# The low-half matmul of logits and index scores on 128 rows of the partitions

## The chip, the cores and the metric

The kernel runs on one core of one Trainium2 chip. The metric is the device time of one execution in microseconds (us); lower is better. The engines are called as in the profile: PE is the matmul engine (TensorE) and PEld its weight loads, DVE is VectorE, ACT is ScalarE, POOL is GpSimd, SP is the engine that issues most DMAs.

## The reference, cut to what matters

One decoder layer over x of 512 tokens by 2048. One input projection feeds three mixers and their gates; then an output projection, a LayerNorm, a gated convolution MLP and a second LayerNorm. All of it is float32.

- DSA: 8 heads of 64. An indexer with 16 heads of 64 scores every query against every earlier key: the sum over heads of weight x relu(query . key). The 128 greatest scores of a row select the keys that the softmax may use.
- S5: a diagonal state space scan over 32 groups, then a gated linear unit.
- MoBA: 8 heads of 64. At this length each query sees its own block of 256 and all past ones, so it is a causal softmax.
- Both softmaxes add a T5 relative bias, one row of a table for each head and distance.

```
rel    = relu(einsum('bqhd,bsd->bqhs', q_idx, k_idx))
score  = einsum('bqh,bqhs->bqs', w_idx, rel)
logits = einsum('bqhd,bshd->bhqs', q, k) * scale + bias
```

## The kernel before

Every matrix product runs in float32r with operands split in two: v = h + l, where h is v rounded to float32r (written by ScalarE) and l = v - h (written by VectorE). A full product is three matmuls, h.h + h.l + l.h (`mm3`, L91 to L93).

Heads of 64 leave half of the 128 partitions free, and the kernel uses them for a shorter form. `q_stacks` makes for a pair of heads the tiles sa and sb: in one half of the partitions the high half of a query, in the other its low half. `k_stacks` makes ka and kb, in which the high half of a key stands on both halves of the partitions, so that one matmul over 128 rows gives h.h + l.h. The remaining h.l is a second matmul over 64 rows into the same bank: only the half of the stack that holds the high half of the query, against the low half of the key in the tile kl. kl holds the low half of head A on partitions 0 to 63 and that of head B on 64 to 127.

`logits` does this for one head and four query tiles of 128 tokens, which see 128, 256, 384 and 512 keys (L438, L440). In DSA a third matmul adds the mask of the selected keys in bf16 (L442), except for the first tile. Each result lies in a bank of the ring "at" (3 banks), is reduced with the bias strip by VectorE (L444) and exponentiated by ScalarE (L446). The strips come by a DMA from a table in DRAM, fdr, that `t5_rows` writes once, when the S5 stage has given its memory free.

`dsa_index` does the same for 16 index heads and three query tiles (L641, L642). All of them share one key, which stands in kia (high half, on both halves of the partitions) and kil (low half, on both halves as well).

The tiles of `q_stacks` and `k_stacks`, and the inputs of S5, share a ring, qp, of six tiles [128, 512]. A pair of softmax heads takes five of them: sa, sb, ka, kb, kl.

The stages follow each other: input transposes, the projections of DSA and S5, index scores, selection of keys (`dsa_topk`, on VectorE), S5, MoBA, DSA, branch products and gates, output projection, MLP. Gate products are put between the parts of the mixers (`gates_ahead`), so that PE has work while the other engines have the mixers'. A planner orders each engine's instructions ahead of the run, from estimated durations and priorities; at run time each engine takes its own in that order. Weights stream on SP's queue; their splits have raised priority.

Of the kernel before, what the change touches and what calls it, by code (L numbers as in the profile page):

```python
# [9 lines left out]
F32 = mybir.dt.float32  # L10
F32R = mybir.dt.float32r
# [5 lines left out]
DRAM = bass.MemoryType.DRAM  # L17
RIGHT = "right"

P = 128  # L20
T = 512
# [7 lines left out]
BIG = 1e30  # L29
HP = 2000  # L30
WK = 11
# gates computed ahead after each part of the mixers
# [7 lines left out]
def tile_trunk(ctx: ExitStack, tc: tile.TileContext, x, rel_bias, w_in, cq_gain, ckv_gain,  # L40
# [3 lines left out]
    nc = tc.nc  # L44
# [50 lines left out]
    # W as the stationary operand: out[col tile] = W[:, cols]^T @ X^T, 512 tokens wide  # L95
# [16 lines left out]
    # 128 columns at the same place of both halves of a matrix's columns  # L112
# [37 lines left out]
    def s5_pow_e(pool, y, name):  # L150
        # e^y to the last bit or so: y = k ln2 + r, a polynomial in r, 2^k from the exponent bits
        sh = list(y.shape)
        n_ = [0]

        def tl(dt=F32):
            n_[0] += 1
            return pool.tile(sh, dt, tag=f"pe{n_[0]}", name=f"pe{n_[0]}")
        v = nc.vector
        yc, k, r, p, e = tl(), tl(), tl(), tl(), tl()
        ki = tl(mybir.dt.int32)  # L160
        v.tensor_scalar(yc, y, -87.0, 88.0, op0=ALU.max, op1=ALU.min)
        v.tensor_scalar(k, yc, 1.4426950408889634, 12582912.0, op0=ALU.mult, op1=ALU.add)
        v.tensor_scalar(k, k, -12582912.0, None, op0=ALU.add)
        v.scalar_tensor_tensor(r, k, -0.693359375, yc, op0=ALU.mult, op1=ALU.add)
        v.scalar_tensor_tensor(r, k, 2.12194440054690583e-4, r, op0=ALU.mult, op1=ALU.add)
        v.tensor_scalar(p, r, 1.0 / 5040, None, op0=ALU.mult)
        for c in (1.0 / 720, 1.0 / 120, 1.0 / 24, 1.0 / 6, 0.5, 1.0):
            v.scalar_tensor_tensor(p, p, c, r, op0=ALU.add, op1=ALU.mult)
        v.tensor_scalar(k, k, 127.0, 8388608.0, op0=ALU.add, op1=ALU.mult)
        v.tensor_copy(ki, k)  # L170
        v.scalar_tensor_tensor(e, p, 1.0, ki.bitcast(F32), op0=ALU.add, op1=ALU.mult)
        return e

    s5 = mside.enter_context(ExitStack())
    sp = right(s5, "sp")
    lhsB = sp.tile([96, 4, 2, 4, P], F32R, name="lhsB")      # h, h, l; q, re/im, G, state
# [9 lines left out]
    def s5_params():  # L186
        v = nc.vector
# [26 lines left out]
        # sine and cosine by half angles after reduction to [-pi, pi]  # L214
# [28 lines left out]
        # (lam_bar - 1) / lam  # L243
# [22 lines left out]
        # input matrices, block-diagonal over the two groups of a pair, inputs on partitions  # L266
# [27 lines left out]
        # output matrices with the states on partitions  # L294
# [12 lines left out]
        # e^{i theta t}, t < 32  # L307
# [59 lines left out]
    fdr = dr.tile([16, 23, 640], F32, name="fdr")  # L367

    def t5_rows():
        with tc.using_default_side(RIGHT), tc.tile_pool(name="t5", bufs=1, reuse_waits="tile") as t5:  # L370
            oh = t5.tile([32, 640], F32, name="oh")
            nc.sync.dma_start(oh, onehot)
            rb = t5.tile([32, 16], F32, name="rb")
            nc.sync.dma_start(rb, rel_bias)
            fr = t5.tile([16, 640], F32, name="fr")
            tb = tp_bank()
            nc.tensor.matmul(tb[:16, :512], rb, oh[:, 0:512], start=True, stop=True)
            nc.vector.tensor_copy(fr[:, 0:512], tb[:16, :512])
            nc.vector.memset(fr[:, 512:640], BIG)
            # 23 copies of a row, so that steps of one row less 1 or 16 elements walk back in distance  # L380
            nc.sync.dma_start(fdr, fr[:, None, :].to_broadcast([16, 23, 640]))

# [17 lines left out]
    def k_stacks(bank):  # L400
        ka = qp.tile([P, T], F32R, tag="q", name="ka")
        kb = qp.tile([P, T], F32R, tag="q", name="kb")
        kl = qp.tile([P, T], F32R, tag="q", name="kl")
        nc.scalar.activation(ka[0:64], bank[0:64], AF.Copy)
        nc.scalar.activation(kb[64:128], bank[64:128], AF.Copy)
        nc.vector.tensor_sub(kl[0:64], bank[0:64], ka[0:64].bitcast(F32))
        nc.vector.tensor_sub(kl[64:128], bank[64:128], kb[64:128].bitcast(F32))
        nc.vector.tensor_copy(ka[64:128], ka[0:64].bitcast(F32))
        nc.vector.tensor_copy(kb[0:64], kb[64:128].bitcast(F32))
        return ka, kb, kl  # L410

    def v_store(bank, t):
        # bank [128 tok, 256 = (pair, A/B, 64)]
        src = bank.rearrange("p (a c d) -> p a c d", a=2, c=2)
        nc.scalar.activation(vh[:, t, :, 0::2, :], src, AF.Copy)
        nc.vector.tensor_sub(vl[:, t, :, 0::2, :], src, vh[:, t, :, 0::2, :].bitcast(F32))
# [3 lines left out]
    def logits(head, hd, qs, kst, mask):  # L420
        # normalised softmax rows of one head, the four query tiles side by side
        ka, kb, kl = kst
        s = qs[hd]
        kk = (ka, kb)[hd]
        half = slice(64 * hd, 64 * hd + 64)
# [8 lines left out]
        for i in range(NT):  # L434
            W = P * (i + 1)
            lb = at_bank()
            qi = slice(i * P, (i + 1) * P)
            nc.tensor.matmul(lb[:, :W], s[:, qi], kk[:, :W], start=True, stop=False)  # L438
            mk = mask is not None and i > 0
            nc.tensor.matmul(lb[:, :W], s[half, qi], kl[half, :W], start=False, stop=not mk)  # L440
            if mk:
                nc.tensor.matmul(lb[:, :W], identb, mask[i], start=False, stop=True)  # L442
            p_ = pt[:, POFF[i]:POFF[i] + W]
            nc.vector.tensor_tensor_reduce(p_, lb[:, :W], strip[:, 384 - i * P:384 - i * P + W],  # L444
                                           1.0, 3e38, ALU.add, ALU.min, mn[:, i:i + 1])
            nc.scalar.activation(p_, p_, AF.Exp, bias=mn[:, i:i + 1], scale=-1.0,  # L446
                                 accum_out=sm[:, i:i + 1])
# [36 lines left out]
    def u_split(G):  # L484
        # the stacked rows h, l, h of a pair of groups meet h, h, l of its matrices
        h, l = w2k("uh", dt=F32R), w2k("ul", dt=F32R)
        split(h, l, oT[1, G])
        us = [qp.tile([P, T], F32R, tag="q", name="us") for _ in range(4)]
        for q in range(4):
            for j, t_ in enumerate((h, l, h)):  # L490
                nc.sync.dma_start(us[q][32 * j:32 * j + 32].bitcast(F32), t_[32 * q:32 * q + 32].bitcast(F32))
        return us

    def s5_tile(G):
# [44 lines left out]
        # 2 gelu(y) in its tanh form  # L539
# [7 lines left out]
    def s5_glu():  # L547
        # 4 times the branch's output: (2 gelu) * (1 + tanh(z/2))
# [24 lines left out]
    def rms_apply(banks, gains, dst, width):  # L573
        # dst = c * gain * (mean(c^2) + eps)^-0.5; the mean token-major, then spread over the partitions
# [25 lines left out]
    def dsa_in():  # L600
# [6 lines left out]
        # index keys on both partition halves; index weights token-major  # L607
# [14 lines left out]
    # value at (p, m) stands for the distance p + 384 - m  # L622
# [5 lines left out]
    def dsa_index(gs):  # L628
        wq2 = w_qidx[0].rearrange("r h d -> r (h d)")
        for g in gs:  # L630
            banks = gemm_w(wq2, (256 * g, 256 * g + 256), cqT, kq=3)
            for pr in range(2):
                qs = q_stacks(banks[pr], 0.125)
                for hd in range(2):
                    h = 4 * g + 2 * pr + hd
                    half = slice(64 * hd, 64 * hd + 64)
                    for i in range(1, NT):
# [4 lines left out]
                        nc.tensor.matmul(lb[:, :W], qs[hd][half, qi], kil[half, :W], start=False, stop=True)  # L642
# [6 lines left out]
    def dsa_topk():  # L649
        # exactly the 128 greatest scores of a row, the lower index first among equals  # L650
# [48 lines left out]
    def moba_v(g):  # L699
        # two token tiles share a bank: its flags are cleared once, by the first of them  # L700
# [42 lines left out]
    qp = mx.enter_context(tc.tile_pool(name="qp", bufs=6, reuse_waits="tile"))  # L743
# [77 lines left out]
    # merged (gates carried twice the sigmoid)  # L821
# [47 lines left out]
    for c, (c0, n) in enumerate(CH):  # L869
# [14 lines left out]
        # the last columns token tile by token tile, so that LayerNorm follows behind  # L884
# [47 lines left out]
    # the accumulator of the down projection starts as alpha * x1  # L932
# [20 lines left out]
    def up_tile(j):  # L953
        if j == 0:
            # in token halves, the first ready before the second
# [37 lines left out]
    def down_last(grp, acts):  # L993
        # token tile by token tile, LayerNorm 2 behind each
# [59 lines left out]
def _bucket_onehot():  # L1054
    # -1 at the T5 bucket of the distance 511 - column (32 buckets, greatest distance 128)
# [32 lines left out]
```

## Time and profile before

| | |
|---|---|
| runs of the kernel before | 2831.72, 2834.8, 2835.8 us; median 2834.8 |
| profiled execution | span 2832.9 us from first to last instruction; no other time of its own is on record |
| mean granted clock of PE | 0.994 of full speed |
| PE busy | 2792.6 us, 99% |
| VectorE busy | 1449.3 us, 51% |
| ScalarE busy | 889.5 us, 31% |
| GpSimd busy | 224.5 us, 8% |

Matmuls overlap: a matmul's recorded duration reaches from its start to its modelled end, past the start of the next. What a stream of matmuls costs is therefore read from the distances between starts. The granted clock is a share of full speed; 0.5 is the lower of its two levels.

### The profile page before, as it was taken

What the parts mean: (1) busy time and instruction counts of PE and PEld (TensorE: products, weight loads), DVE (VectorE), ACT (ScalarE), POOL (GpSimd) and SP (SyncE); (2) the same over time, 40 slices, a digit from 0 to 9 for tenths busy, and PEclk for the clock granted to TensorE, in tenths of its full rate; (3) what the DMA queues carried; (4) which work ended last, traced back from release to release, by engine and by line L of the source; (5) the groups of instructions that cost most, each with busy time, mean ns of one, the idle gap of its engine ahead of it and who ended that gap; (6) DMA issues with size and microseconds to landing.
All of it is one profiled execution on the core that took longest, in us unless ns stands there. A gap on an engine that the chain in (4) does not pass through costs nothing.

```text
span 2832.9 us, 32264 instructions
## 1 busy us (share of the span) xinstructions
PE 2792.6 (99%) x12651; PEld 2255.8 (80%) x12655; DVE 1449.3 (51%) x2176; ACT 889.5 (31%) x1325; POOL 224.5 (8%) x163
## 2 busy tenths in 40 slices
PE   9999999999999999999899999999999999999998
PEld 7777877777887778889778888888888888888886
DVE  6357988885445446434553334333433333333448
ACT  3243333334344432212532232331322322322321
POOL 0000011110000003100420000000000000000002
PEclk9999999999999999999999999999999999999999
DMA  6223433334332335533433333333333333323333
GB/s 199 84 80 93 127 108 118 117 89 93 82 98 86 96 126 192 168 119 105 134 104 97 97 97 92 99 94 94 97 97 97 97 97 97 97 90 97 97 97 112
DMA packets 352824, 301.82 MB, mean 107 GB/s; under 512 B 20963, under 2 KB 307600, under 8 KB 352160
## 3 DMA queue, kind: packets, MB, share of 16 engines
q1 hardware_dynamic: 339536, 281.44, 33.2%
q10 hardware_dynamic: 10832, 14.12, 1.4%
q0 software_dynamic: 2304, 4.20, 0.6%
q8 instruction: 99, 1.62, 0.2%
q14 instruction: 53, 0.43, 0.0%
HBM read 278.31 MB, written 18.24 MB: 105 GB/s over the span
## 4 chain that ended last, share of the span: by engine, by line
PE 94%; DVE 3%; DMA 1%; issue 1%; POOL 1%; ACT 0%; DVEq 0%; SPq 0%; ACTq 0%; POOLq 0%
PE mmb L91 24%; PE mmb L93 23%; PE mmb L92 23%; PE atb L93 4%; PE atb L92 4%; PE atb L91 4%; PE avb L93 2%; PE avb L91 2%; PE avb L92 2%; PE atb L440 1%; PE atb L642 1%; PE atb L460 1%; PE mmb L711 1%; PE avb L536 1%; PE mmb L712 1%
## 5 line engine op out<-in xcount | busy, mean ns | idle before, releaser
L73 DVE TENSOR_TENSOR wl<-raw,wh 128x1024 fp32r<-128x1024 f32 (+1 forms) x468 | 601.1, 1285 | 946.6 <-ACT wh L72 930.2
L72 ACT ACTIVATE wh<-raw 128x1024 fp32r<-128x1024 f32 (+1 forms) x468 | 489.1, 1045 | 1364.1 <-PE mmb L92 905.0
L91 PE MATMUL mmb<-x1h,wh 128*128 128x512 f32 (+1 forms) x1440 | 552.7, 385 | 5.4 <-ACT wh L72 5.4
L92 PE MATMUL mmb<-x1l,wh 128*128 128x512 f32 (+1 forms) x1440 | 555.5, 386 | 1.6 <-DVE x1l L917 1.6
L93 PE MATMUL mmb<-x1h,wl 128*128 128x512 f32 (+1 forms) x1440 | 526.1, 385 | 6.8 <-DVE wl L73 6.8
L91 PE MATMUL mmb<-xh,wh 128*128 128x512 f32 (+1 forms) x1056 | 419.6, 398 | 1.2 <-ACT wh L72 1.2
L92 PE MATMUL mmb<-xl,wh 128*128 128x512 f32 (+1 forms) x1056 | 418.9, 397 | 0.0
L93 PE MATMUL mmb<-xh,wl 128*128 128x512 f32 (+1 forms) x1056 | 407.5, 397 | 0.6 <-DVE wl L73 0.6
L93 PEld LDWEIGHTS mmb<-x1h,wl 128*128 128x128 f32 x1440 | 270.9, 188 | 61.6 <-DVE wl L73 8.0
L91 PEld LDWEIGHTS mmb<-x1h,wh 128*128 128x128 f32 x1440 | 270.0, 188 | 60.0 <-ACT wh L72 6.3
L92 PEld LDWEIGHTS mmb<-x1l,wh 128*128 128x128 f32 x1440 | 271.3, 188 | 56.8 <-DVE x1l L917 2.6
L91 PEld LDWEIGHTS mmb<-xh,wh 128*128 128x128 f32 (+1 forms) x1056 | 199.3, 189 | 54.7 <-issue 9.0
L93 PEld LDWEIGHTS mmb<-xh,wl 128*128 128x128 f32 (+1 forms) x1056 | 198.7, 188 | 52.7 <-issue 9.4
L92 PEld LDWEIGHTS mmb<-xl,wh 128*128 128x128 f32 (+1 forms) x1056 | 199.1, 189 | 47.4 <-issue 6.9
L93 PE MATMUL atb<-wh,al 128*128 128x512 f32 x480 | 189.8, 395 | 0.0
L92 PE MATMUL atb<-wl,ah 128*128 128x512 f32 x480 | 189.5, 395 | 0.0
L949 DVE SCALAR_TENSOR_TENSOR cv<-mmb,cwc,cv 128x511 f32<-128x511 f32 (+1 forms) x176 | 131.6, 748 | 88.0 <-ACT cv L947 84.8
L91 PE MATMUL atb<-wh,ah 128*128 128x512 f32 x480 | 170.7, 395 | 0.0
L970 POOL TENSOR_TENSOR cv<-cv 128x512 f32<-128x512 f32 x44 | 57.7, 1311 | 1251.7 <-DVE cv L949 1251.7
L93 PEld LDWEIGHTS atb<-wh,al 128*128 128x128 f32 x480 | 89.9, 187 | 22.1
L91 PEld LDWEIGHTS atb<-wh,ah 128*128 128x128 f32 x480 | 90.0, 187 | 21.9
L92 PEld LDWEIGHTS atb<-wl,ah 128*128 128x128 f32 x480 | 90.0, 187 | 21.7
(369 smaller groups left out, 3342.6 us busy)
## 6 DMA issues: line engine op xcount, KB each, us to landing
raw<-in_w_up_dram SPq DMA_DIRECT2D x360, 256.0 KB, 3.4
raw<-in_w_in_dram SPq DMA_DIRECT2D x120, 512.0 KB, 3.7
raw<-in_w_down_dram SPq DMA_DIRECT2D x88, 512.0 KB, 3.6
raw<-in_w_out_dram SPq DMA_DIRECT2D x32, 512.0 KB, 3.7
raw<-in_w_branch_dram SPq DMA_DIRECT2D x24, 512.0 KB, 4.6
thd<-th ACTq DMA_DIRECT2D x22, 512.0 KB, 2.9
th<-thd SPq DMA_DIRECT2D x22, 512.0 KB
raw<-in_w_in_dram SPq DMA_DIRECT2D x32, 256.0 KB, 3.4
```

What stands on the lines that cost most here:

```text
L72: nc.scalar.activation(wh, raw, AF.Copy)
L73: nc.vector.tensor_sub(wl, raw, wh.bitcast(F32))
L91: nc.tensor.matmul(o, ah, bh, start=start, stop=False)
L92: nc.tensor.matmul(o, ah, bl, start=False, stop=False)
L93: nc.tensor.matmul(o, al, bh, start=False, stop=stop)
L440: nc.tensor.matmul(lb[:, :W], s[half, qi], kl[half, :W], start=False, stop=not mk)
L460: nc.tensor.transpose(tb[:, (i - j) * P:(i - j + 1) * P], pt[:, o:o + P], ident)
L536: nc.tensor.matmul(yb[rw], ctr[:, G, rw], t[0], start=True, stop=False, tile_position=(0, 32 * q))
L642: nc.tensor.matmul(lb[:, :W], qs[hd][half, qi], kil[half, :W], start=False, stop=True)
L711: nc.tensor.matmul(o, xh[:, ts_], wl[:, k], start=False, stop=False, skip_group_check=True)
L949: nc.vector.scalar_tensor_tensor(c_[:, s_:], bank[:, :T - s_], cwc[:, j * 88 + f:j * 88 + f + 1], c_[:, s_:], op0=ALU.mult, op1=ALU.add)
L970: nc.gpsimd.tensor_mul(ca, ca, cv)
```

## The change

The low half of the key is put on both halves of the partitions too. In `k_stacks`, kl becomes two tiles, la and lb, each filled on its second half by one more copy on VectorE. The second matmul of each logit then takes the whole stack of the query, over 128 rows, against la or lb. The second matmul of each index score takes the whole stack against kil, which already stands on both halves. So l.l is added to each product as well. The ring qp gets a seventh tile. The remaining lines of the diff only take out comments.

```
 def k_stacks(bank):
     ka = qp.tile([P, T], F32R, tag="q", name="ka")
     kb = qp.tile([P, T], F32R, tag="q", name="kb")
-    kl = qp.tile([P, T], F32R, tag="q", name="kl")
+    la = qp.tile([P, T], F32R, tag="q", name="la")
+    lb = qp.tile([P, T], F32R, tag="q", name="lb")
     nc.scalar.activation(ka[0:64], bank[0:64], AF.Copy)
     nc.scalar.activation(kb[64:128], bank[64:128], AF.Copy)
-    nc.vector.tensor_sub(kl[0:64], bank[0:64], ka[0:64].bitcast(F32))
-    nc.vector.tensor_sub(kl[64:128], bank[64:128], kb[64:128].bitcast(F32))
+    nc.vector.tensor_sub(la[0:64], bank[0:64], ka[0:64].bitcast(F32))
+    nc.vector.tensor_sub(lb[64:128], bank[64:128], kb[64:128].bitcast(F32))
     nc.vector.tensor_copy(ka[64:128], ka[0:64].bitcast(F32))
     nc.vector.tensor_copy(kb[0:64], kb[64:128].bitcast(F32))
-    return ka, kb, kl
+    nc.vector.tensor_copy(la[64:128], la[0:64].bitcast(F32))
+    nc.vector.tensor_copy(lb[0:64], lb[64:128].bitcast(F32))
+    return (ka, kb), (la, lb)
...
 def logits(head, hd, qs, kst, mask):
-    ka, kb, kl = kst
-    s = qs[hd]
-    kk = (ka, kb)[hd]
-    half = slice(64 * hd, 64 * hd + 64)
+    s, kk, kl = qs[hd], kst[0][hd], kst[1][hd]
...
-        nc.tensor.matmul(lb[:, :W], s[half, qi], kl[half, :W], start=False, stop=not mk)
+        nc.tensor.matmul(lb[:, :W], s[:, qi], kl[:, :W], start=False, stop=not mk)
...
 def dsa_index(gs):
...
-        nc.tensor.matmul(lb[:, :W], qs[hd][half, qi], kil[half, :W], start=False, stop=True)
+        nc.tensor.matmul(lb[:, :W], qs[hd][:, qi], kil[:, :W], start=False, stop=True)
...
-qp = mx.enter_context(tc.tile_pool(name="qp", bufs=6, reuse_waits="tile"))
+qp = mx.enter_context(tc.tile_pool(name="qp", bufs=7, reuse_waits="tile"))
```

## Rows read from the trace of the kernel before

**Rows 1.** The page's busy times: us, share of the span, instructions.
```profile
PE 2792.6 (99%) x12651; PEld 2255.8 (80%) x12655; DVE 1449.3 (51%) x2176; ACT 889.5 (31%) x1325; POOL 224.5 (8%) x163
```

**Rows 2.** Line L440: duration in ns min/median/max, first and last start.
```profile
L440 PE MATMUL atb<-kl,sa x32: 322/409/792, 638.9 to 959.9; 64*128 64x128 f32 x8, 64*128 64x256 f32 x8, 64*128 64x384 f32 x8, 64*128 64x512 f32 x8
```

**Rows 3.** Windows: length, then us busy of PE, PEld, DVE, ACT, POOL; clock, DMA.
```profile
150.00:250.00 100.00, 100.00 (x380) 69.67 (x380) 53.74 (x80) 43.63 (x75) 0.00 (x0) 1.00 0.25 73
250.00:330.00 80.00, 80.00 (x354) 66.15 (x353) 77.51 (x184) 22.78 (x33) 2.55 (x2) 1.00 0.44 131
...
720.00:800.00 80.00, 80.00 (x451) 68.42 (x449) 31.34 (x61) 27.90 (x52) 2.35 (x4) 1.00 0.33 91
```

**Rows 4.** Timeline of the matmul engine, first index head: start us, duration us.
```profile
148.87 0.28 PE L641 MATMUL atb<-kia,sa 128*128 128x256 f32 x1
149.08 0.38 PE L642 MATMUL atb<-kil,sa 64*128 64x256 f32 x1
...
150.99 0.50 PE L91 MATMUL mmb<-cqh,wh 128*128 128x512 f32 x1
151.33 0.39 PE L92 MATMUL mmb<-cql,wh 128*128 128x512 f32 x1
151.56 0.39 PE L93 MATMUL mmb<-cqh,wl 128*128 128x512 f32 x1
```

**Rows 5.** Timeline of the matmul engine, MoBA values and projections.
```profile
728.12 0.33 PE L93 MATMUL avb<-ph,vl 128*128 128x384 f32 x1
728.29 0.28 PE L711 MATMUL mmb<-wl,xh 128*128 128x256 f32 x1
728.40 0.28 PE L712 MATMUL mmb<-wh,xl 128*128 128x256 f32 x1
...
730.56 0.22 PE L91 MATMUL avb<-ph,vh 128*128 128x128 f32 x1
730.62 0.33 PE L712 MATMUL mmb<-wh,xl 128*128 128x256 f32 x1
```

**Rows 6.** Timeline of the matmul engine, one MoBA pair alone.
```profile
703.82 0.40 PE L438 MATMUL atb<-kb,sb 128*128 128x512 f32 x1
...
704.91 0.39 PE L92 MATMUL mmb<-yl,wh 128*128 128x512 f32 x1
```

**Rows 7.** Timeline of the matmul engine, one DSA pair with its mask.
```profile
888.65 0.28 PE L438 MATMUL atb<-kb,sb 128*128 128x256 f32 x1
...
889.53 0.40 PE L92 MATMUL mmb<-xl,wh 128*128 128x512 f32 x1
```

**Rows 8.** Timeline of the matmul engine, behind its wait in MoBA.
```profile
656.26 0.79 PE L438 MATMUL atb<-ka,sa 128*128 128x512 f32 x1 [4.75 <-DVE mn L444]
...
658.30 0.63 PE L91 MATMUL mmb<-xh,wh 128*128 128x512 f32 x1
658.72 0.63 PE L92 MATMUL mmb<-xl,wh 128*128 128x512 f32 x1
```

**Rows 9.** Window behind that wait, columns as in rows 3.
```profile
656.00:665.00 9.00, 8.74 (x19) 5.91 (x20) 6.01 (x19) 4.45 (x13) 0.00 (x0) 0.51 0.43 118
```

**Rows 10.** Chain that ended last, in order of time: start us, us, what.
```profile
637.11 0.69 DVE kl L407
...
639.17 0.58 DVE fr L378
...
639.78 11.29 DMA fdr<-fr
...
651.67 4.22 DMA strip<-fdr
```

**Rows 11.** VectorE's groups of instructions, 600 to 1000 us: busy us, mean ns.
```profile
L409 DVE CAST kb<-kb 64x512 fp32r<-64x512 f32 x8 | 3.4, 423 | 0.2
```

**Rows 12.** Timeline of VectorE, last key copy of the second DSA pair.
```profile
860.26 0.42 DVE L409 CAST kb<-kb 64x512 fp32r<-64x512 f32 x1
```

**Rows 13.** Timeline of the matmul engine, first logit of that pair.
```profile
876.42 0.30 PE L438 MATMUL atb<-ka,sa 128*128 128x128 f32 x1
```

More of the change, by code (lines that the diff above doesn't have):

```diff
@@ L635, in dsa_index @@
                     h = 4 * g + 2 * pr + hd
-                    half = slice(64 * hd, 64 * hd + 64)
                     for i in range(1, NT):
```

## The prediction

> **What bounds the kernel now.** I read the page's busy times first: the matmul engine is busy for 2792.6 of 2832.9 us and VectorE for half of it [rows 1]. A busy matmul engine is not one at its peak, so I next took start-to-start distances between matmuls from the timeline, since what the change can give is a distance that is longer than it has to be. Then the windows by stage: in stretches where the changed code runs the matmul engine is never idle (100.00 of 100.00 us in the index scores, 80.00 of 80.00 in MoBA), nor where VectorE is nearly full between them, 77.51 of 80.00 us in the selection of keys [rows 3]. Program order on this engine is fixed, so a matmul that ends sooner brings everything behind it forward, unless another engine's result is then late. The chain of waits names the one place where that happens today, the start of the MoBA logits [rows 10].
>
> **Part 1, the second matmul goes from 64 to 128 rows.** There are 64 logit pairs, L438 and L440 (the row counts the 32 of one of the two head tiles) [rows 2], and by the code 16 x 3 = 48 index pairs, L641 and L642; 112 in all.
>
> What an undisturbed 128-row matmul of each width takes, start to start: 0.06 us for 128 columns, 0.11 to 0.12 for 256, 0.17 for 384 [rows 5] and 0.23 for 512 (151.33 to 151.56) [rows 4]. I take 0.06, 0.12, 0.17, 0.23.
>
> An index head is three pairs, widths 256, 384, 512, back to back. From its first matmul to the second one behind it the trace takes 151.33 - 148.87 = 2.46 us [rows 4]. Without disturbance the same seven matmuls would take 2 x (0.12 + 0.17 + 0.23) + 0.23 = 1.27. Of the 1.19 us too much, the first step shows 0.21 where 0.12 is due (0.09: the 64-row matmul waits for the 128-row one to leave), and the last shows 0.34 where 0.23 is due (0.11: the weights, which otherwise load under the matmul before, load alone). Six changes of row count at 0.09 + 0.11 = 0.20 make 1.2. The other 15 heads repeat it at 2.45 to 2.47 us, with no wait for data in them. **Index: 16 x 1.2 = 19.2 us.**
>
> A logit pair that stands alone takes 704.91 - 703.82 = 1.09 us to the second matmul behind it, where 3 x 0.23 = 0.69 is due: 0.40 [rows 6]. With a mask matmul behind it, it is 889.53 - 888.65 = 0.88, where 3 x 0.12 + 0.23 = 0.59 is due: 0.29, say 0.30 [rows 7]; the mask itself shows no delay of its own. So:
> DSA: 8 pairs without mask at 0.40 and 24 with at 0.30, 10.4 us.
> MoBA: of 32 pairs, 26 at 0.40, 10.4 us. Three more run at the half clock: the first takes 658.30 - 656.26 = 2.04 us where three matmuls at that clock (658.72 - 658.30 = 0.42 each) need 1.26, so 0.78; for the two shorter ones, not opened here, I take 0.6 each; 2.0 us [rows 8]. The granted clock there is 0.51, the 1.2 GHz level, after the engine had stood idle [rows 8, 9]. The last three pairs run before that idle time and give nothing (part 2).
> **Sum of part 1: 19.2 + 10.4 + 10.4 + 2.0 = 42.0 us.**
>
> Does a 128-row second matmul cost more itself? The trace has the same shape as the first matmul of the pair, in the undisturbed distances above, so nothing for that. A bf16 mask right behind a 128-row matmul of 32-bit data is not in the trace: between 0 and 0.1 us for each of 24 (the load alone was 0.11 above), at most 2.4 us; I take 0, as the matmul after the mask loads early today.
>
> A rule speaks against the 0.11. The Trainium skill ("TensorE: Matmul & The Clock Gate", Part 3, "What overlaps and what doesn't") lets a weight load overlap a running matmul only when the two use different row groups; two 128-row matmuls share all of them. This trace does not agree: the distances of 0.23 for 512 columns in [rows 4] leave no 0.11 for a load. By the rule the sum would be that of the second rival below.
>
> **Part 2, two more copies in each k_stacks.** The new la and lb copies have the form of the CAST of L409, 0.42 us [rows 11]: 8 x 2 x 0.42 = 6.8 us of VectorE. Seven of the eight sets lie beside matmuls in stretches like 720 to 800, where VectorE is busy 31.34 of 80 us [rows 3], and long ahead of use: the last copy of the second DSA pair ends at 860.68, its first logit starts at 876.42 [rows 12, 13], 15.7 us of cover. Without that cover each set would cost 0.84. Queued behind the copies on VectorE are the high-half and low-half splits of weights, but these have a unit of 24 matmuls (24 x 0.23 = 5.5 us) ahead of them.
>
> The first MoBA set has no cover. VectorE works without a break from the subtraction kl (637.11) to the copy fr of L378 (639.17), which the bias table's DMA waits for (11.29 us), which the strip's DMA waits for (4.22), which the first reduction waits for, and that frees the logits bank for the matmul at 656.26 [rows 10, 8]. The matmul engine stands idle 4.75 us for it. Two copies ahead of L378 put 0.84 us onto the end. If the planner puts them behind L378, it is 0; I take 0.84, since the other k copies stand ahead of it. For the same reason the three pairs before the wait give nothing: the engine gets there 0.9 us sooner and waits 0.9 longer. The S5 stage before, 19.2 us sooner as a whole, brings the table's DMA forward with it, because VectorE starts its selection of keys from the last index score, and the matmul engine is full there too [rows 3].
>
> **Part 3, a seventh buffer in qp.** Six tiles of seven now belong to a pair where five of six did: one is free for the next pair, before and after. It costs 2 KB a partition and no time. What it does to the planner's order can't be read here; I put 0 in the sum and keep it for the range.
>
> **Sum:** 42.0 - 0.8 = 41.2 us off the span of 2832.9, so 2791.7. The median of the runs stands 1.9 us above that span, so **2793.6 us**.
>
> **The rivals.**
> 1. New waits take part of it. The logits' results go through VectorE and ScalarE and come back as transposes; with the pairs 0.3 to 0.4 us shorter, the engine may reach a bank or a normalised row too early. Against it: today the matmul engine waits almost nowhere there. If half of the 22.8 us of the logits is lost, 2793.6 + 11.4 = 2805; if all, 2816.
> 2. The drain goes but the load stays exposed. 224 changes at 0.11 are 24.6 us, so 2793.6 + 24.6 = 2818. Against it: the undisturbed distances.
> 3. The gap does not come from the row count, but, say, from the low-half tile being read or both matmuls writing one bank. Then nothing is saved and the copies stay: 2834.8 + 0.8 = 2835.6, no change. Against it: three matmuls into one bank run at 0.23 everywhere else.
> 4. Slower: the key stacks come late. With six tiles for a pair, and its four copies as the last work on VectorE, the stacks of a pair could end after the matmul engine wants them. It decides from the point where the 15.7 us of cover are used up [rows 12, 13]; beyond, each us costs one, and an idle time like that at 656 also brings 9 us at 0.51 of the clock [rows 9], some 4.4 us. To pass the 41 us gained, six of the pairs must each be 2.5 us and more beyond the cover: 6 x (2.5 + 4.4) = 41. For it: only that these copies wait for banks and buffers too. About 2840.
>
> **How the numbers follow.** Forecast 0.70; rival 1 0.12; rival 2 0.06; rival 3 0.04; rival 4 0.05; more gained than worked out (the idle time at 651 or the slow clock behind it shrinks, some 9 us: 4.75 of the wait and 4.4 of the clock) 0.03. The forecast's own range: 2788 (masked pairs at 0.40 give 2.4, the copies hidden 0.8, the rest for the order) to 2800 (mask 2.4, and 4 for waits). For 8 in 10 it must take in most of rival 1: 2785 to 2815. Faster by over 0.2% (5.7 us, about what a measurement of this kernel can tell from none): 0.70 + 0.12 + 0.06 + 0.03 = 0.91; within it 0.04; slower 0.05.
>
> **What would show it.** Right: the six matmuls of an index head 1.27 us apart instead of 2.46, the index stage 19 us shorter; no 64-row matmul left, and their weight loads starting under the matmul before; the idle time before the first MoBA logits longer, 4.75 + 0.9 + 0.8 = 6.4 us; the DSA logits ending about 41 us sooner and everything behind at the same distances as before. Wrong: idle time of the matmul engine in the logits released by VectorE or ScalarE (rival 1), loads of 0.19 us that begin only when the matmul before has ended (rival 2), distances unchanged (rival 3), the first logits of a DSA pair waiting for la or lb (rival 4), or the queues in another order, with idle time in places that have none today.

## Result and the profile after

| kernel | median | runs | ratio to the kernel before, 95% interval |
|---|---|---|---|
| changed, first time | 2802.53 us | 4 | 0.9888 [0.9874, 0.9902] |
| changed, beside the later experiments | 2802.89 us | 4 | 0.9886 [0.9871, 0.9900] |

The kernel before took 2833.98 us beside the first and 2836.21 beside the second. The change saves 31.5 to 33.3 us, 1.1%; 41.2 were forecast. The time lies 8.9 us above the stated one, inside the stated range (2785 to 2815) and 2.5 us outside the narrower one that the forecast gave itself (2788 to 2800).

The page after, busy times as in [rows 1]; the matmul engine is busy for 98% of a shorter span, so the work itself became shorter:

```profile
PE 2756.6 (98%) x12655; PEld 2254.9 (81%) x12655; DVE 1472.5 (53%) x2192; ACT 886.2 (32%) x1325; POOL 223.6 (8%) x163
```

The first index head after the change, timeline of the matmul engine as in [rows 4] (the index lines are now L640 and L641, those of the logits stay L438 and L440):

```profile
149.59 0.28 PE L640 MATMUL atb<-kia,sa 128*128 128x256 f32 x1
149.71 0.28 PE L641 MATMUL atb<-kil,sa 128*128 128x256 f32 x1
...
150.86 0.39 PE L92 MATMUL mmb<-cql,wh 128*128 128x512 f32 x1
```

And the weight loads of the same stretch, behind them one of the kernel before, of the 64-row matmul at 149.08 in [rows 4]:

```profile
149.59 0.19 PEld L641 LDWEIGHTS atb<-kil,sa 128*128 128x128 f32 x1
149.72 0.19 PEld L640 LDWEIGHTS atb<-kia,sa 128*128 128x128 f32 x1
```

```profile
149.08 0.18 PEld L642 LDWEIGHTS atb<-kil,sa 64*128 64x128 f32 x1 [0.25 <-issue]
```

From the first matmul to the second behind the head it is 150.86 - 149.59 = 1.27 us, where it was 2.46. All distances are those of undisturbed matmuls, and each load of 0.19 us starts with the matmul before its own (149.59 with 149.59, 149.72 with 149.71), so it is hidden. In the kernel before, the load of the 64-row matmul starts only with that matmul itself, at 149.08.

A MoBA pair alone, a DSA pair with mask and a pair 128 wide, three cuts of the timeline. The first two are to be read against [rows 6] and [rows 7], the third against the same place of the kernel before, which stands last:

```profile
691.15 0.39 PE L438 MATMUL atb<-kb,sb 128*128 128x512 f32 x1
...
691.83 0.39 PE L93 MATMUL mmb<-yh,wl 128*128 128x512 f32 x1
```

```profile
851.70 0.28 PE L438 MATMUL atb<-ka,sa 128*128 128x256 f32 x1
851.82 0.28 PE L440 MATMUL atb<-la,sa 128*128 128x256 f32 x1
851.94 0.28 PE L442 MATMUL atb<-mask,identb 128*128 128x256 bf16 x1
851.98 0.48 PE L93 MATMUL mmb<-ckh,wl 128*128 128x512 f32 x1
852.29 0.39 PE L91 MATMUL mmb<-ckh,wh 128*128 128x512 f32 x1
```

```profile
676.83 0.30 PE L438 MATMUL atb<-ka,sa 128*128 128x128 f32 x1
676.98 0.27 PE L440 MATMUL atb<-la,sa 128*128 128x128 f32 x1
677.09 0.45 PE L93 MATMUL mmb<-xh,wl 128*128 128x512 f32 x1
677.37 0.40 PE L91 MATMUL mmb<-xh,wh 128*128 128x512 f32 x1
```

```profile
687.37 0.30 PE L438 MATMUL atb<-ka,sa 128*128 128x128 f32 x1
...
688.19 0.40 PE L92 MATMUL mmb<-xl,wh 128*128 128x512 f32 x1
```

Alone 0.68 us instead of 1.09, with mask 0.59 instead of 0.88: the forecast 0.40 and 0.29. The mask shows no delay behind a 128-row matmul (851.94 - 851.82 = 0.12 in front of it; 852.29 - 851.94 = 0.35 for it and the next, as undisturbed). The 128-wide pair takes 677.37 - 676.83 = 0.54 us instead of 688.19 - 687.37 = 0.82: it gives 0.28, where the forecast took 0.40 for it. By the undisturbed distances it would take 2 x 0.06 + 0.23 = 0.35, so 0.2 us are still lost in it.

So the matmuls gave nearly what was forecast, and most of the missing 8 to 10 us were lost elsewhere. What the matmul engine waited for, over the whole span (us in total, times, longest), names two waits of the mixers, one of them new:

```profile
PE atb L438 <- DVE mn L444: 4.8, 1, 4.8
PE avb L536 <- DVE t L533: 4.2, 1, 4.2
```

L536 is the output matmul of S5. The chain of waits around it, the last S5 pair (start us, us, what):

```profile
605.90 1.94 DVE wl L73
...
607.87 0.74 DVE y L538
...
608.65 1.42 DVE t L527
...
610.07 1.12 DVE t L528
...
611.80 0.69 DVE sa L393
...
614.41 1.13 DVE wl L73
615.54 0.61 DVE t L533
...
616.20 1.29 PE avb L536 x2
```

VectorE has the whole way: the split of a weight unit, the output of the pair before, two scans, then the query stack sa of MoBA's first pair (L393), more products, another split. The matmul engine has done all that stands ahead of this product at 612.0 and waits 4.21 us; behind the wait its granted clock is low:

```profile
617.00:626.00 9.00, 9.00 (x29) 6.05 (x29) 4.94 (x12) 0.59 (x1) 0.00 (x0) 0.82 0.22 64
```

A granted clock of 0.82 over 9 us is 1.6 us more. In the kernel before no wait stands there.

A second loss stands behind the last logits of DSA. Two waits for the splits of a weight, 1.23 and 0.62 us, are in the kernel before as well; only here the clock is low behind them. The window of the changed kernel, and the same one of the changed kernel with a ring of six (an experiment below):

```profile
968.40:971.80 3.40, 3.40 (x9) 2.66 (x9) 0.84 (x1) 0.00 (x0) 0.00 (x0) 0.51 0.74 205
```

```profile
960.90:964.30 3.40, 3.40 (x15) 2.78 (x16) 0.93 (x1) 0.00 (x0) 0.00 (x0) 1.00 0.65 188
```

That is 1.7 us more. All four profiles with a ring of seven have this stretch, and none of the six with a ring of six. The question is then: has S5 become VectorE's stage because the index scores are faster, or has the order changed?

Orders answer half of it. The order of each engine's instructions is made before the run. With 128 rows in the index scores alone it is, instruction for instruction, that of the kernel before. With a ring qp of seven and nothing else, the matmul engine's order through the index scores and S5 is already that of the changed kernel. Between the last two S5 output products on L536 stand 51 other matmuls in the kernel before, and 23 in the changed one (those of L537 not counted).

### The profile page after: what moved, and what is told of

Same layout as the page of the kernel before. It is cut to its first block, busy times and chain, and to the rows that moved or that the text cites. A ratio compares the mean times of both kernels' runs of the same rounds, so it can differ in the third digit from the quotient of the medians.

```text
span 2800.5 us, 32275 instructions
## 1 busy us (share of the span) xinstructions
PE 2756.6 (98%) x12655; PEld 2254.9 (81%) x12655; DVE 1472.5 (53%) x2192; ACT 886.2 (32%) x1325; POOL 223.6 (8%) x163
## 4 chain that ended last, share of the span: by engine, by line
PE 94%; DVE 3%; DMA 1%; POOL 1%; issue 1%; ACT 0%; SPq 0%; DVEq 0%; ACTq 0%
PE mmb L93 24%; PE mmb L91 24%; PE mmb L92 24%; PE atb L93 4%; PE atb L92 4%; PE atb L91 4%; PE avb L93 2%; PE avb L91 2%; PE avb L92 2%; DVE wl L73 1%; PE atb L460 1%; PE mmb L710 1%; PE mmb L709 1%; PE mmb L711 1%; PE avb L536 1%
## 5 line engine op out<-in xcount | busy, mean ns | idle before, releaser
L73 DVE TENSOR_TENSOR wl<-raw,wh 128x1024 fp32r<-128x1024 f32 (+1 forms) x468 | 612.3, 1309 | 920.4 <-ACT wh L72 906.4
```

What stands on the lines that cost most here:

```text
L73: nc.vector.tensor_sub(wl, raw, wh.bitcast(F32))
```

## Experiments

Gains are against the kernel before as it ran beside each: 2834.19 us for the first four, 2836.21 for the rest.

**128 rows in the index scores alone**

```
 kernel before, dsa_index:
-nc.tensor.matmul(lb[:, :W], qs[hd][half, qi], kil[half, :W], start=False, stop=True)
+nc.tensor.matmul(lb[:, :W], qs[hd][:, qi], kil[:, :W], start=False, stop=True)
```

> Only the index scores take their second matmul over 128 rows; k_stacks, the logits and the ring of six are as before, and every engine's order of instructions is that of the kernel before. Both theories: an index head takes 1.28 us instead of 2.46, 16 x 1.18 = 18.9 us. Order theory (the 4.4 us that the matmul engine waits before the last S5 matmul of the changed kernel come from the order that the ring of seven brings): no such wait here, 2834.0 - 18.9 = 2815. VectorE theory (S5 comes 19 us sooner and VectorE, nearly full there, can't follow): the wait stands here as well, 4.4 us and about 2 us of slow clock behind it, 2821 to 2822.

Measured 2816.8 us, ratio 0.9931 [0.9916, 0.9946], a gain of 17.4. The matmul engine's waits in it:

```profile
PE mmb L93 <- DVE wl L73: 9.1, 4, 7.1
PE atb L438 <- DVE mn L444: 5.3, 1, 5.3
```

No wait at L536, though S5's first matmul stands at 295.8 us, 18 us sooner than before and 5 sooner than in the changed kernel. The order theory holds, the VectorE theory falls. Of the 1.5 us short of 18.9, 0.5 is the wait before the MoBA logits, 5.3 us here and 4.75 before [rows 8]; the rest is within the spread of the runs.

**The changed kernel with a ring of six**

```
-qp = mx.enter_context(tc.tile_pool(name="qp", bufs=7, reuse_waits="tile"))
+qp = mx.enter_context(tc.tile_pool(name="qp", bufs=6, reuse_waits="tile"))
```

> The changed kernel with six tiles in the ring qp in place of seven. Its order in the index scores and in S5 is that of the kernel before. Order theory: no wait before the last S5 matmul, so it is about 6.5 us faster than the changed kernel, 2796. VectorE theory: the wait stays, 2802. If the ring of six also holds up the stacks of the next pair (all six tiles belong to one pair), the first logits of a pair wait for them: each of 6 pairs could lose some us, and it would be slower than 2802.

Measured 2795.69 us, ratio 0.9857 [0.9842, 0.9871]: 7 us faster than the changed kernel. Its waits, and then the chain that ends the one before the MoBA logits, as in [rows 10]:

```profile
PE mmb L93 <- DVE wl L73: 8.3, 3, 7.1
PE atb L438 <- DVE mn L444: 6.7, 1, 6.7
```

```profile
617.85 0.59 DVE fr L378
...
618.47 11.37 DMA fdr<-fr
...
630.44 6.22 DMA strip<-fdr
...
637.04 0.80 PE atb L438
```

The S5 wait is gone. The last two S5 output products start 608.66 - 594.72 = 13.9 us apart, with 51 other matmuls between them; in the changed kernel it is 616.20 - 604.31 = 11.9, and 4.21 of them are waited. Timelines of the matmul engine, the ring of six and then the changed kernel, and last VectorE's product L533 in the ring of six, which the last output product needs:

```profile
594.72 1.04 PE L536 MATMUL avb<-t,ctr 128*32 128x512 f32 x2
...
608.66 1.04 PE L536 MATMUL avb<-t,ctr 128*32 128x512 f32 x2
```

```profile
604.31 1.04 PE L536 MATMUL avb<-t,ctr 128*32 128x512 f32 x2
...
616.20 1.29 PE L536 MATMUL avb<-t,ctr 128*32 128x512 f32 x2 [4.21 <-DVE t L533]
```

```profile
604.61 0.68 DVE L533 TENSOR_TENSOR t<-t,ta 128x512 f32<-128x512 f32 x1
```

With six tiles VectorE is done with it at 605.29, 10.6 us behind the earlier output product, and the matmul engine comes for it at 608.66, 3.4 us later. With seven, VectorE's own order has changed too (a split ahead of y and the stack sa come first, in the chain above) and it is done at 616.15, 11.8 us behind; and the matmul engine has 28 matmuls less to do meanwhile, 28 x 0.23 = 6.4 us. So 6.4 + 1.2 - 3.4 = 4.2 us are waited.

The wait before the MoBA logits is longer, 6.74 us for 4.75, since the strip's DMA takes 6.22 us where it took 4.22. The copies of la and lb aren't in it, as VectorE's timeline shows, first with the ring of six and then in the changed kernel:

```profile
617.77 0.67 DVE L378 COPY fr<-atb 16x512 f32<-16x512 f32 x1
...
618.80 0.42 DVE L411 CAST la<-la 64x512 fp32r<-64x512 f32 x1
619.25 0.42 DVE L412 CAST lb<-lb 64x512 fp32r<-64x512 f32 x1
```

```profile
620.42 0.42 DVE L412 CAST lb<-lb 64x512 fp32r<-64x512 f32 x1
...
631.70 0.68 DVE L378 COPY fr<-atb 16x512 f32<-16x512 f32 x1 [0.77 <-PE atb L377]
```

With six they stand behind the copy fr of L378 (617.77) that the table waits for. In the changed kernel they stand ahead of it, but 11 us ahead, and VectorE then idles: fr waits for the matmul engine (L377).

**A ring of seven, nothing else**

```
 kernel before:
-qp = mx.enter_context(tc.tile_pool(name="qp", bufs=6, reuse_waits="tile"))
+qp = mx.enter_context(tc.tile_pool(name="qp", bufs=7, reuse_waits="tile"))
```

> The kernel before with seven tiles in the ring qp, nothing else: 64-row second matmuls, three key tiles. Its order in the index scores and in S5 is that of the changed kernel. Order theory: the wait before the last S5 matmul is here too, about 4 us and 2 us of slow clock, 2834.0 + 6.5 = 2840. VectorE theory: index scores are as slow as before, so there is no such wait, 2834.

Measured 2841.02 us, ratio 1.0020 [1.0011, 1.0030]: 6.8 us slower than before. Its index heads take 2.46 us each, and the wait is there:

```profile
PE atb L438 <- DVE mn L444: 4.3, 1, 4.3
PE avb L536 <- DVE t L533: 4.2, 1, 4.2
```

The same 4.2 us with slow index scores: it comes from the order, and the order from the number of buffers. The rest of the loss is clock. In this profile it is at 0.50 from 634.4 to 639.3, behind that wait, and at 0.52 from 1007.9 to 1011.3, behind the DSA logits: 2.5 and 1.6 us. Less 0.5 for the shorter wait before the MoBA logits this makes 7.8, and the profiled spans differ by 2840.5 - 2832.9 = 7.6 us.

**Three 128-row matmuls, then three of 64**

```
 kernel before, dsa_index, each head:
+for i in range(1, NT):    # i: query tile
+    ... matmul(lbs[i][:, :W], qs[hd][:, qi], kia[:, :W], start=True, stop=False)
+for i in range(1, NT):
+    ... matmul(lbs[i][:, :W], qs[hd][half, qi], kil[half, :W], start=False, stop=True)
```

> The kernel before with the six matmuls of an index head in another order: the three over 128 rows first, then the three over 64. Two changes of row count a head in place of six. If each change costs 0.20 us (drain and exposed load), a head takes 1.27 + 2 x 0.20 = 1.67 us. If each 64-row matmul costs its 0.40 us whatever stands beside it, it stays at 2.46. The program's order elsewhere differs from that of the kernel before, so only the distance within a head counts: 16 x 0.8 = 12.6 us less in the index scores by the first.

One run, 2832.88 us, so its time decides nothing. The planner undid the grouping in 15 heads; their order is that of the kernel before. The first head kept it:

```profile
148.92 0.69 PE L642 MATMUL atb<-kia,sa 128*128 128x256 f32 x3
149.54 0.80 PE L646 MATMUL atb<-kil,sa 64*128 64x256 f32 x3
150.27 0.50 PE L91 MATMUL mmb<-cqh,wh 128*128 128x512 f32 x1
150.61 0.39 PE L92 MATMUL mmb<-cql,wh 128*128 128x512 f32 x1
```

It takes 150.61 - 148.92 = 1.69 us, where 1.67 was expected and 2.46 is what an alternating head takes. So the cost belongs to the change of row count, 0.20 to 0.21 us each, and not to the 64-row matmul; one head shows it. As a way to save time it failed.

**128 rows in the logits alone, ring of six**

```
 ring-of-six kernel, dsa_index:
-nc.tensor.matmul(lb[:, :W], qs[hd][:, qi], kil[:, :W], start=False, stop=True)
+nc.tensor.matmul(lb[:, :W], qs[hd][half, qi], kil[half, :W], start=False, stop=True)
```

> Only the logits take their second matmul over 128 rows (la, lb and their copies as in the changed kernel), index scores over 64 rows, ring of six; every engine's order is that of the ring-of-six run. Row theory, from the distances already seen there: 26 MoBA pairs and 32 DSA pairs give about 0.35 us each and three slow-clock pairs 0.6, together 22, less what the pairs before the wait for the strip can't give: 2834.2 - 21 = 2813. If the gains of the two halves hinder each other, the sum of both kernels' gains (17.4 of the index scores alone, and this one's) is not the 38.5 of the ring-of-six run.

Measured 2817.0 us, ratio 0.9935 [0.9919, 0.9952], a gain of 19.2. With the 17.4 of the index scores that makes 36.6, where the ring of six with both gained 38.5: they add up within the spread of the runs (4 us in each set). 21 was expected; the difference is inside the spread as well.

**The bias table made early**

```
 ring-of-six kernel:
 for g in range(2):
     s5_u(g)
+t5_rows()
...
 s5.close()
-t5_rows()
```

> The ring-of-six kernel with the bias table made and written to DRAM right after the projections, long before S5, instead of after S5. If the matmul engine's wait before the first MoBA logits (6.74 us there, and some 4 us of slow clock behind it) is due to the table's DMA alone, both go and the time falls by about 10 us from 2795.7, to 2786. If the strips, the split of weights or VectorE's work at the hand-over would hold it up anyway, a wait of some us stays: 2790 to 2796.

Measured 2787.14 us, ratio 0.9828 [0.9814, 0.9843], the fastest of all, 8.5 us less than the ring of six by the times, 10.6 by the gains. The matmul engine's longest waits are now those on weights and on the input; the line of L438 is gone:

```profile
PE mmb L93 <- DVE wl L73: 6.7, 4, 2.8
PE mmb L91 <- ACT wh L72: 6.4, 3, 4.0
PE atb L339 <- DMA xi<-in_x_dram: 4.8, 2, 3.9
```

So the wait before the MoBA logits was the table's DMA alone. While it stands, matmuls made shorter between the table's DMA and this point should only lengthen it; that is argued from the chain, and no run shows it by itself.

**The changed kernel once more**

> The changed kernel once more, beside the others on one chip: 2802 to 2803, if the difference of 6.8 us to the ring of six is one of the kernels and not of the chips.

Measured 2802.89 us, ratio 0.9886 [0.9871, 0.9900], against 0.9857 [0.9842, 0.9871] with the ring of six: the intervals only touch. Its profile has the 4.2 us wait at L536 and the low clock behind the DSA logits again.

**The changed kernel with 64 rows**

```
 changed kernel, logits and dsa_index:
-... s[:, qi], kl[:, :W] ...
+... s[half, qi], kl[half, :W] ...
-... qs[hd][:, qi], kil[:, :W] ...
+... qs[hd][half, qi], kil[half, :W] ...
```

> The changed kernel (la and lb with their copies, ring of seven) with both second matmuls taken over 64 rows again. Against the run with the ring of seven alone it has the copies more: 2841 if they are hidden, 2842 if 0.84 us stand on the way to the bias table, 2845 and more if each of the eight sets costs. Against the changed kernel it shows what the 128 rows are worth in this order: about 39 us, 18.9 of the index scores and 20 of the logits.

Measured 2841.18 us, ratio 1.0021 [1.0011, 1.0030]. Against the ring of seven alone (2841.02), the copies cost 0.2 us, nothing that can be measured. Against the changed kernel, the 128 rows are worth 2841.18 - 2802.89 = 38.3 us; the runs of the two sets spread over 6.4 and 5.2 us. In the two profiles the way from the first index matmul to the last second matmul of a logit is 824.3 and 783.9 us, 40.4 apart. The matmul engine's order is that of the changed kernel up to the end of MoBA; in DSA it differs in places.

## Why the prediction was right, and where it was not

**Part 1 was right in mechanism and nearly in size.** Forecast 42.0 us; 38.3 measured by the runs, 40.4 by the profiles. The index scores: 19.2 forecast, 16 x 1.18 = 18.9 by the distances. The logits: the pairs alone and those with a mask gave 0.41 and 0.29 in the cuts above. The sixteen 128-wide pairs were taken at the 0.40 of a 512-wide one and gave 0.28 in the two places where both kernels have neighbours of the same shapes; if all of them did, 16 x 0.12 = 1.9 us are missing. The 0.06 us distance, read where one such matmul stood among wider ones, does not hold for two in a row (0.15 and 0.11).

**The rule on weight loads.** The Trainium skill ("TensorE: Matmul & The Clock Gate", Part 3, "What overlaps and what doesn't") lets a load overlap a running matmul only when their row groups differ. The trace contradicts it: 128-row loads start with the 128-row matmul before their own, 149.59 with 149.59. Rival 2 is out, as the distances are the undisturbed ones, and so is rival 3, as they changed.

**Part 2.** The copies are hidden altogether, and the 0.8 us were not paid. The prediction read VectorE as working without a break up to the copy fr of L378; in the changed order it idles there, so copies 11 us ahead of fr cost nothing, and in the ring of six they stand behind it. Rival 4 did not show.

**Part 3 is the step that failed:** "It costs 2 KB a partition and no time", and 0 in the sum. The seventh buffer changes the order that the planner makes. Ahead of the last S5 output product the matmul engine then has 28 matmuls less, 6.4 us of work that used to fill the time until VectorE had its operand, and VectorE has it 1.2 us later. This costs 6.8 us on the kernel before: 4.2 of wait, and the rest with the slow clock, in part right behind it and in part behind the DSA logits. It is most of the 8 to 10 us that are missing. The prediction had named an order with idle time in new places among its signs of being wrong, without a price. That the time still lies in the stated range is in part luck: its upper end was set for rival 1, whose loss did not come. Rival 1 had the right kind of loss in the wrong place: a new wait for VectorE, in S5 and not in the logits, and not from the pairs being shorter. Without the seventh buffer the forecast of 41.2 us meets 38.5 measured.

**The wait before the logits.** In the ring of six it is 6.74 us, and 6.4 were forecast, but that is luck: the strip's DMA, 2.0 us longer, accounts for all of the difference, and not the copies. Why it took longer is open. In the changed kernel the wait is 4.8, as before.

What is left open is why the planner's estimates favour that order with seven buffers, and why the clock falls behind the DSA logits only then; the runs show that both happen, and what they cost.

## What to carry to other kernels

On a full matmul engine, look at the distances between starts for places where the row count changes from one matmul to the next: each change cost 0.20 us here, and doubling the operand over the idle partitions removes it. The spare work that pays for this can be free, but a spare buffer is an instruction to the planner too: compare the order of instructions with and without it, and try the change with the ring left as it was. Where an engine waits for a DMA chain, gains ahead of it may vanish there, so start that chain earlier first.

## What the runs showed of the hardware

- A change between 64 and 128 rows costs 0.20 to 0.21 us at the 2.4 GHz clock, about 0.09 of it in front of the matmul with the new row count, read as the one before leaving the array, and 0.11 behind it, whose weight load starts only with it (149.08 with 149.08). That it goes with the number of changes (six a head 1.19 us, two 0.42) was not known before the run with the first head grouped.
- A 128-row float32r matmul with new weights costs 0.23 us for 512 columns and 0.12 for 256, but a pair of 128-wide ones 0.26 us together where it stands between other tiles (676.83 to 677.09). The loads there start 0.11 us apart (676.81, 676.92, 677.03 on PEld).
- Behind the wait of 4.2 us in S5 the matmul engine ran at the lower clock, 1.2 GHz: 512 columns took 0.43 us until 620.2, then 0.23. Behind waits of 1.23 and 0.62 us at the end of DSA the clock was low in all four profiles with a ring of seven (0.51 from 968.4 to 971.8) and full in all six with a ring of six (1.00 from 960.9 to 964.3).
